# Triangles by ranges of chunks, the product of r and k on VectorE, and a chunk of the recurrence in three blocks

## The chip, the cores and the metric

One Trainium2 chip, one core. The metric is the device time in microseconds (us) of one execution; the kernel before takes 2971.76 us (median of 3 runs, 2968.67 to 2973.62). Engines are named as in the profile: PE (TensorE; PEld are its weight loads), DVE (VectorE), ACT (ScalarE), POOL (GpSimd), SP (the queue that issues most transfers; ACT and POOL issue some of theirs).

## What is computed

One inference step of a two-layer decoder: an RWKV-7 layer and a latent-attention layer, on 1024 prompt tokens and 8 sample tokens. The change touches the first layer alone: its keys and decays, and its recurrence over time.

```python
mixed = h[None] + dx[None] * mix[:4, None, None, :]
r, k, v, z = jnp.einsum('pbtd,pde->pbte', mixed, w_in)
w_log = -jax.nn.softplus(-(w0 + jnp.tanh(xw @ w1) @ w2)) - 0.5
decay = jnp.exp(-jnp.exp(w_log.astype(F32)))
a = jax.nn.sigmoid(a0 + (xa @ a1) @ a2)
kk = heads(k * k_k)                                # then normalised per head
k = k * (1 + (a - 1) * k_a)
...
def _wkv_step(S, inp):
    r, w, k, v, a, b = inp
    sa = jnp.einsum('bhvk,bhk->bhv', S, a)
    S = S * w[:, :, None, :] + sa[..., None] * b[:, :, None, :] + v[..., None] * k[:, :, None, :]
    return S, jnp.einsum('bhvk,bhk->bhv', S, r)
...
bonus = (jnp.sum(rh * kh * r_k, axis=-1, keepdims=True) * vh)
out = ((yn + bonus) * jax.nn.silu(z)) @ w_out
```

There are 32 heads of 64 channels (2048 in all), so 16 tiles of 128 channels hold two heads each. The kernel does the recurrence in 32 chunks of 32 tokens; within a chunk a 32x32 unit triangular matrix per head must be inverted ("the triangle"), and that inverse is the matrix U below.

## The kernel before

**The loop over k** (inside `phase_a`, span 480 to 960 us). `for ct in range(KI - 1)` goes over the 16 tiles. In turn `ct` PE projects k of the tile after (`kproj`, 24 steps of three matmuls p<-mh,w1h / ml,w1h / mh,w1l), projects the decay and the rate (`ua`, six pairs u<-th,l2h and u<-th,l2l, the second over 64 rows alone), forms sums of squares (`norm`, ss), the products inside a chunk of the tile before (`score`, sc), transposes (`rows`, tr) and the bonus (`bonus`, bo<-K,rkb). DVE makes the running decays by two scans (`decay2`, L797 and L798: Wp and its inverse Wi), the new key (`newkey`, L806 to L808) and the scaled rows RA and BK (`raw_rows`, `unit`, `unit2`, `unit_rows`, L813 to L830). The low parts of the split weights come from L76 (w1l on DVE here). POOL forms K<-R,GG, the product of r and the new key (L821), which `bonus` reads in the next turn. Program order is the order of every engine's queue; PE, DVE, ACT and POOL each run theirs in order.

**The triangles.** `inverse(q, ...)` solves eight packs: pack q holds the four heads of tiles 2q and 2q+1 for all 32 chunks, as 128 partitions (head, chunk). It has 31 steps of a product (Xt<-N,X, L1081) and a sum (X<-X,Xt, L1083) over up to 256 elements. `steps` gives one step of the open pack after three of four steps of `kproj`; seven packs run on POOL, one pack per two tiles, and the eighth on DVE after the loop. The results go to `u_d` and, for the last two, to `u2_d`.

**The seam** (960 to 1034 us). After the last `score`, PE has 24 steps of the z projection (`zg`) around the last rows, the transposes boT of the bonus, 27 more z steps, and then rh of chunk 0. DVE splits the mixed rows ml and solves the eighth triangle; POOL stores it.

**The recurrence** (`phase_r`). `for c in range(NC)` has six blocks per chunk: rh (X by state), sa (U by rhs), new_state (s), outs (y), for the first and the second half of the heads (`rh(c,0)`, `new_state(c-1,1)`, `sa(c,0)`+`outs(c-1,1)`, `rh(c,1)`, `new_state(c,0)`, `sa(c,1)`+`outs(c,0)`), each followed by `fill(w)`, which puts in z steps at an even rate so that PE has work while ACT and DVE move the block's result. `load(c+2)` brings the chunk's rows: `xs_d` on SP (64 rows, 16 pieces of 512 bytes each) and `ra_d` on ACT (pieces of 256 bytes). `out_block` normalises four chunks' output, a step per block. `sample_step` does the eight sample tokens on POOL and DVE, one step per block, with the state S fetched and stored in 16 parts.

Of the kernel before, what the change touches and what calls it, by code (L numbers as in the profile page):

```python
# [21 lines left out]
P = 128  # L22
# [33 lines left out]
def tile_yoco(ctx, tc, A, O, dbg=None):  # L56
# [30 lines left out]
    xs_d = scr("xs_d", (2, NC, 64, P * KI))  # L87
# [4 lines left out]
    n_d = scr("n_d", (KI, 2, NC, C, C))  # L92
    mz_d = scr("mz_d", (KT, P, T))
    u_d = scr("u_d", (NC, 4, C, 6, C))
    u2_d = scr("u2_d", (NC, 2, 4, C, C))
# [102 lines left out]
    def phase_a():  # L198
        with ExitStack() as px:
# [15 lines left out]
            shT = lp.tile([P, KT, NB], F32, name="shT")  # L215
# [3 lines left out]
            omx = hp.tile([P, 48], F32, name="omx")  # L219
            w1x = px.enter_context(ExitStack())  # L220
# [399 lines left out]
            Wi = kp.tile([P, NC, 33], F32, name="Wi")  # L620
            E0 = kp.tile([P, NC, 33], BF16, name="E0")
# [6 lines left out]
            G.memset(E0, 0.0)  # L628
            G.memset(E0[:, :, 0:1], 1.0)
# [16 lines left out]
            def wcut(i, ct, hf):  # L646
# [8 lines left out]
                lo(b_, raw[:, 4 * hf:4 * hf + 4], a)  # L655
# [7 lines left out]
            def lora(ct):  # L663
                raw = kp.tile([P, P], F32, tag="l2r", name=f"l2r{ct}")
                SY.dma_start(raw[0:64], A["a_w2"][0][:, ts(ct, P)])
                SY.dma_start(raw[64:128], A["a_a2"][0][:, ts(ct, P)])
                st[ct]["l2r"] = raw

            def lcut(ct):
                raw = st[ct]["l2r"]  # L670
                s2 = st[ct]["s2"] = [kp.tile([P, P], F32R, tag=f"l2h{i}", name=f"l2h{i}_{ct}", bufs=2) for i in range(2)]
                l2 = st[ct]["l2"] = kp.tile([P, P], F32R, tag="l2l", name=f"l2l{ct}", bufs=2)
                for i in range(2):
                    me = slice(64 * i, 64 * i + 64)
# [8 lines left out]
            def ua(ct):  # L683
# [3 lines left out]
                for i, dst in enumerate((d["TW"], d["TA"])):  # L687
                    me = slice(64 * i, 64 * i + 64)
                    for n in range(3):
                        p_ = kbank(f"u{i}_{ct}_{n}")  # L690
                        mm(p_[:, :NQ], d["s2"][i], th2[i][:, nsl[n]], True, False)
                        mm(p_[:, :NQ], d["l2"][me], th2[i][me, nsl[n]], False, True)
# [84 lines left out]
            def norm(ct):  # L777
                d = st[ct]
                RN = d["RN"] = kp.tile([P, T], F32, tag="RN", name=f"RN{ct}")
                for n in range(3):  # L780
                    p_ = kbank(f"ss{ct}_{n}")
                    mm(p_[:, :NQ], blk, d["SQ"][:, nsl[n]], True, True)
                    V.tensor_scalar(RN[:, nsl[n]], p_[:, :NQ], 1e-24, None, ALU.max)
                ACT.activation(RN, RN, AF.Ln)
                ACT.activation(RN, RN, AF.Exp, scale=-0.5)

            def decay(ct):

# [12 lines left out]
            def newkey(ct):  # L801

                d = st[ct]
                TA = d["TA"]
                GG = d["GG"] = kp.tile([P, T], F32, tag="GG", name=f"GG{ct}", bufs=2)
                V.tensor_scalar(GG, TA, dv[:, 2, ct:ct + 1], dv[:, 3, ct:ct + 1], ALU.mult, ALU.add)  # L806
                V.tensor_scalar(TA, TA, -0.5, -0.5, ALU.mult, ALU.add)
# [1965 lines left out]
```

## Time and profile before

| | |
|---|---|
| median of the runs | 2971.76 us |
| the profiled execution | 2943.64 us |
| its span, first to last instruction | 2941.9 us |
| mean granted TensorE clock | 0.957 |
| PE busy | 2696.3 us, 92% |
| DVE busy | 1672.7 us, 57% |
| POOL busy | 1430.5 us, 49% |
| ACT busy | 1361.2 us, 46% |

PE is busy for 92% of the span, so what can be gained lies where it is not, and the stages differ: the same engines are read by stretches further down. A busy share of PE holds time at the lower clock too; a stretch with PEclk below 1 has both idle time and slower matmuls. "Idle before, releaser" names what ended an idle time.

### The profile page before, as it was taken

How to read it: one execution, taken by the hardware profiler on the slowest of the kernel's cores; microseconds unless marked ns; L12 is line 12 of the kernel's file. 1: busy time of each engine (PE TensorE's matmuls, PEld its weight loads, DVE VectorE, ACT ScalarE, POOL GpSimd, SP SyncE). 2: the span in 40 equal slices, each digit the busy share in tenths (PEclk: the TensorE clock that was granted, in tenths of full speed). 3: DMA queues.
4: the chain of work that ended last, by engine and by line, in shares of the span. 5: the costliest groups of instructions: out<-in, count | busy, mean ns of one | idle time of the engine just before them, and what ended most of it. 6: DMA issues, size and time to landing. Idle time of an engine off the chain costs nothing.

```text
span 2941.9 us, 64866 instructions
## 1 busy us (share of the span) xinstructions
PE 2696.3 (92%) x26386; PEld 2418.5 (82%) x26386; DVE 1672.7 (57%) x2952; ACT 1361.2 (46%) x2886; POOL 1430.5 (49%) x1385
## 2 busy tenths in 40 slices
PE   7999998878786788888879999999999999899998
PEld 7999997766675677767769989999999999666897
DVE  7232117989797756666574144127777777533414
ACT  7232226767675444445454335225555555333423
POOL 3322121699999566663245455313444433475342
PEclk9999999989898899999989999999999999999999
DMA  4332334667677899999777552322111111586525
GB/s 157 120 126 76 96 88 113 162 145 174 155 162 190 206 223 218 227 227 210 175 228 225 173 123 78 107 83 83 54 56 54 56 52 55 157 274 201 179 90 187
DMA packets 567501, 423.80 MB, mean 144 GB/s; under 512 B 176260, under 2 KB 515649, under 8 KB 567074
## 3 DMA queue, kind: packets, MB, share of 16 engines
q1 hardware_dynamic: 473954, 336.06, 42.5%
q10 hardware_dynamic: 79648, 38.42, 4.9%
q0 software_dynamic: 13600, 45.16, 4.9%
q8 instruction: 208, 3.41, 0.5%
q14 instruction: 91, 0.75, 0.1%
HBM read 281.69 MB, written 133.35 MB: 141 GB/s over the span
## 4 chain that ended last, share of the span: by engine, by line
PE 57%; POOL 7%; DVE 7%; DMA 5%; issue 4%; ACT 3%; SPq 1%; ACTq 0%; DVEq 0%; POOLq 0%
PE p L62 8%; PE zb L62 6%; PE sc L62 6%; PE bo L62 5%; PE wop L62 4%; PE o L62 4%; POOL Xt L1081 2%; POOL X L1083 2%; PE s L62 2%; PE q L62 2%; PE pt L2156 2%; PE v L62 2%; PE k L62 1%; PE pt L2575 1%; PE bt L62 1%
## 5 line engine op out<-in xcount | busy, mean ns | idle before, releaser
L76 POOL TENSOR_TENSOR wl<-wr,wh 128x1024 fp32r<-128x1024 f32 x32 | 84.3, 2654 | 288.0 <-ACT wh L71 269.5
L1081 POOL TENSOR_TENSOR Xt<-N,X 128x31 f32<-128x31 f32 (+15 forms) x217 | 187.0, 862 | 27.2 <-DMA N<-n_d 11.0
L1083 POOL TENSOR_TENSOR X<-X,Xt 128x31 f32<-128x31 f32 (+15 forms) x217 | 183.8, 847 | 17.0
L71 ACT CAST pth<-pt 128x256 fp32r<-128x256 f32 (+1 forms) x320 | 108.2, 355 | 128.8 <-DVE ptl L76 74.8
L1289 DVE TENSOR_TENSOR st<-s,gC 64x512 f32<-64x512 f32 x128 | 88.2, 689 | 131.6 <-PE s L62 129.2
L62 PE MATMUL p<-mh,w3h 128*128 128x344 f32 x384 | 149.6, 390 | 6.2 <-issue 5.0
L76 DVE TENSOR_TENSOR ptl<-pt,pth 128x256 fp32r<-128x256 f32 (+1 forms) x320 | 120.9, 391 | 27.0 <-ACT pth L71 25.0
L62 PE MATMUL p<-ml,w3h 128*128 128x344 f32 x384 | 130.8, 341 | 5.1 <-issue 2.9
L62 PE MATMUL p<-mh,w1h 128*128 128x344 f32 x360 | 134.9, 375 | 0.0
L62 PE MATMUL p<-mh,w3l 128*128 128x344 f32 x384 | 127.1, 337 | 3.7 <-issue 3.7
L62 PE MATMUL r<-mh,wh 128*128 128x344 f32 x384 | 124.7, 325 | 4.6 <-ACT tf L483 4.6
L62 PE MATMUL r<-mh,wl 128*128 128x344 f32 x384 | 124.1, 323 | 0.0
L62 PE MATMUL r<-ml,wh 128*128 128x344 f32 x384 | 123.9, 323 | 0.0
L2139 ACT ACTIVATE pr<-sc,mx 128x128 f32<-128x128 f32 (+7 forms) x128 | 95.4, 745 | 53.1 <-DVE mx L2136 51.6
L62 PE MATMUL p<-mh,w1l 128*128 128x344 f32 x360 | 119.9, 333 | 0.0
L62 PE MATMUL p<-ml,w1h 128*128 128x344 f32 x360 | 119.8, 333 | 0.0
L2136 DVE TENSOR_REDUCE mx<-sc 128x1 f32<-128x128 f32 (+7 forms) x128 | 96.7, 755 | 3.2
L1305 ACT COPY y<-y 32x256 f32<-32x256 f32 x256 | 93.2, 364 | 10.7 <-PE y L62 7.1
L1276 ACT COPY st<-sa 32x256 f32<-32x256 f32 x128 | 46.4, 362 | 111.1 <-PE sa L62 100.7
L1950 DVE TENSOR_TENSOR zbr<-zb,RS 128x384 f32<-128x384 f32 (+1 forms) x48 | 24.6, 515 | 126.1 <-PE zb L62 123.8
L62 PEld LDWEIGHTS s<-st,xz 128*64 128x64 f32 x2048 | 72.6, 148 | 27.9 <-issue 20.9
L2041 POOL TENSOR_TENSOR qp<-qp,rope 128x256 f32<-128x256 f32 (+1 forms) x30 | 22.4, 747 | 145.8 <-DMA qsw<-qp 122.4
(1237 smaller groups left out, 9944.9 us busy)
## 6 DMA issues: line engine op xcount, KB each, us to landing
xs_d<-XS SPq DMA_DIRECT2D x64, 512.0 KB, 5.9
xz<-xs_d SPq DMA_DIRECT2D x64, 512.0 KB, 9.0
wr<-in_a_w_in_dram SPq DMA_DIRECT2D x17, 1024.0 KB, 6.1
ra_d<-RA SPq DMA_DIRECT2D x32, 512.0 KB, 7.3
xz<-ra_d ACTq DMA_DIRECT2D x58, 256.0 KB, 7.4
rT_d<-rr ACTq DMA_DIRECT2D x16, 516.0 KB, 2.6
R<-rT_d SPq DMA_DIRECT2D x16, 516.0 KB, 3.5
w3r<-in_a_w_in_dram SPq DMA_DIRECT2D x16, 512.0 KB, 6.2
```

Of the source, the lines that this page charges most:

```text
L62: PE.matmul(out, lhsT=lhsT, rhs=rhs, start=start, stop=stop)
L71: ACT.copy(out, in_)
L76: (eng or V).tensor_tensor(out, in_, hi_.bitcast(F32), ALU.subtract)
L1081: eng.tensor_tensor(t3, N_[:, s_:s_ + 1, s_ + 1:].to_broadcast([P, a, b]), X_[:, r0:r1, s_:s_ + 1].to_broadcast([P, a, b]), ALU.mult)
L1083: eng.tensor_tensor(X_[:, r0:r1, s_ + 1:], X_[:, r0:r1, s_ + 1:], t3, ALU.add)
L1276: (V.tensor_copy if j % 2 else ACT.copy)(d, pa[j % 2][ts(j, 32)])
L1289: V.tensor_tensor(ST[s_][1 - c % 2][rows, qs, :], p3[rows], gC[rows, qs, c:c + 1].to_broadcast([64, 8, 64]), ALU.mult)
L1305: ACT.copy(ys[B][ts(ci, 32), a:a + 2].rearrange("p a s d -> p (a s d)"), p_[ts(j, 32), 0:256])
L2136: V.tensor_reduce(mx, sc[:, :W], AX.X, ALU.max, negate=True)
L2139: ACT.activation(pr[:, :W], sc[:, :W], AF.Exp, bias=mx, accum_out=sm)
L2156: PE.transpose(pt[:, ts(q, P)], pr[:, ts(g + q, P)], ident)
L2575: PE.transpose(p_[:, ts(r, P)], pg[:, r, ts(c, P)], ident)
```

## The change

1. **Loop.** r times k goes from POOL to DVE (`rk`, after `unit_rows`); the low part of w1 goes from DVE to POOL. One scan of the summed exponents (CS) takes the place of two, and ACT makes Wp, Wi and gC by Exp; ACT makes the factor of `newkey`; the rate's affine step is folded into `unit2` and `unit_rows`. The second matmul of `ua` reads 128 rows (both halves of th), from doubled raw weights. `rows` copies a transposed bank once (TR) and no longer eight times per pair. The parts of a turn stand in another order; the end of `decay2` and `newkey` now stands at the end of the turn before.
2. **Triangles.** Tiles 0 to 7 stay packs over all chunks, two packs to an instruction, on POOL from turns 4 and 8 at 0.36 steps per z or k step. Tiles 8 to 15 are packs over eight chunks: chunks 0 to 15 on DVE after the loop (two packs to an instruction), chunks 16 to 31 on POOL during the recurrence (`side`), ahead of the sample step.
3. **Scratch.** `xs_d` is two tensors, by tile; a store writes rows of 2 or 4 KB, a load reads pieces of 256 bytes, four loads per chunk on SP in place of two. `u2_d` holds four tensors, stored by 16 transfers each: for the first by SP and ACT in turn, for the second by POOL.
4. **Recurrence.** Three blocks per chunk, with `fill(2.0)` each (6.0 per chunk, as before). The output block has two steps per block; the side work two, and three from chunk 12 on.

```diff
@@ lora, lcut, ua
-                raw = kp.tile([P, P], F32, tag="l2r", name=f"l2r{ct}")
+                raw = kp.tile([P, 2, P], F32, tag="l2r", name=f"l2r{ct}")
...
-                        mm(p_[:, :NQ], d["l2"][me], th2[i][me, nsl[n]], False, True)
+                        mm(p_[:, :NQ], d["l2"][:, i], th2[i][:, nsl[n]], False, True)
@@ wcut
-                lo(b_, raw[:, 4 * hf:4 * hf + 4], a)
+                lo(b_, raw[:, 4 * hf:4 * hf + 4], a, G if i == 1 else V)
@@ decay, decay2
+                ACT.activation(CS[:, :, 1:33], c3(TW), AF.Identity, bias=ones[:, 0:1])
...
-                V.tensor_tensor_scan(fl(Wp), fl(Wp), fl(E0), 0.0, ALU.mult, ALU.add)
-                V.tensor_tensor_scan(fl(Wi), fl(Wi), fl(E0), 0.0, ALU.mult, ALU.add)
-                V.tensor_copy(gC[:, ct, :], Wp[:, :, 32])
+                V.tensor_tensor_scan(fl(CS), fl(E0), fl(CS), 0.0, ALU.mult, ALU.add)
+                ACT.activation(fl(Wp), fl(CS), AF.Exp, scale=-0.5 * CDEC)
+                ACT.activation(Wi, CS[:, :, 1:33], AF.Exp, scale=0.5 * CDEC)
+                ACT.activation(gC[:, ct, :], CS[:, :, 32], AF.Exp, scale=-0.5 * CDEC)
@@ newkey, unit, rk
-                V.tensor_scalar(GG, TA, dv[:, 2, ct:ct + 1], dv[:, 3, ct:ct + 1], ALU.mult, ALU.add)
-                V.tensor_scalar(TA, TA, -0.5, -0.5, ALU.mult, ALU.add)
+                ACT.activation(GG, st[ct]["TA"], AF.Identity, bias=dv[:, 3, ct:ct + 1], scale=dv[:, 2, ct:ct + 1])
-                G.tensor_tensor(d["K"][:, :S], d["R"][:, :S], d["GG"][:, :S], ALU.mult)
+                V.tensor_tensor(d["K"][:, :S], d["R"][:, :S], d["GG"][:, :S], ALU.mult)
@@ rows
-                for u in range(2):
-                    src = slice(64 * u, 64 * u + 64)
-                    ACT.copy(x4[64:128, :, u, :], v4[src, :, 0, :])
-                    ACT.copy(x4[0:64, :, u, :], v4[src, :, 1, :])
+                ACT.copy(d["TR", hf][:, :, ts(g % 2, 4)], p_.rearrange("p (m s d) -> p s m d", m=4, s=2))
...
+                        SY.dma_start(xs_d[1][s_, ct][:, HC[hf]], d["XS", hf][64 * s_:64 * s_ + 64])
+                        for u in range(2):
+                            SY.dma_start(xs_d[0][1 - s_, ct][:, c0 + 8 * u:c0 + 8 * u + 8], d["TR", hf][ts(u, 64), s_])
@@ the loop
+            GROUPS = {4: [(0, 0), (0, 1)], 8: [(0, 2), (0, 3)]}
+            def whole(qs, eng=G):
...
+                rate[0] = 0.36
@@ after the loop
-            iv7 = inverse(KI // 2 - 1, ivb, [(V, 0, C)], late)
-            next(iv7)
+            iv7 = whole([(1, 0), (1, 1)], V)
...
@@ inverse, store
+                            {0: (SY, ACT), 1: (G, G)}.get(q, (SY, SY))[j % 2].dma_start(u2_d[q][:, j, :, x], X_[rows, i])
@@ phase_r, load
-                    SY.dma_start(X[rows, :, 128 - 128 * s_:256 - 128 * s_], xs_d[s_, c].rearrange("r (a t) -> r a t", t=P))
+                    for i, x in enumerate((c // 16 * 16 + c % 2 * 8 + c % 16 // 2, c)):
+                        SY.dma_start(X[rows, :, o + 64 * i:o + 64 * i + 64], xs_d[i][s_, :, :, x].rearrange("a r t -> r a t"))
@@ phase_r, the chunks
-                for i in range(6):
+                for i in range(3):
...
-                    fill(1.4 if i % 3 == 2 else 0.8)
+                    run(take(sg, 3 if c > 11 else 2))
+                    fill(2.0)
```

On POOL in the middle of the loop, before: each product of r and k (L821, K) stands among the steps of a pack of triangles (N, X, Xt).

```order
L1081 TENSOR_TENSOR Xt_5662<-N_5660,X_5661 128x256
L1083 TENSOR_TENSOR X_5661<-X_5661,Xt_5662 128x16x16
L1081 TENSOR_TENSOR Xt_5662<-N_5660,X_5661 128x255
L1083 TENSOR_TENSOR X_5661<-X_5661,Xt_5662 128x17x15
L821 TENSOR_TENSOR K_5452<-R_5695,GG_5841 128x1024
L1081 TENSOR_TENSOR Xt_5662<-N_5660,X_5661 128x252
```

The same place now: a step covers two packs, and what stands among the steps is the low part of the weights of the next k tile (w1l).

```order
L1107 TENSOR_TENSOR Xt_6907<-N_6905,X_6906 128x440
L1109 TENSOR_TENSOR X_6906<-X_6906,Xt_6907 128x2x22x10
L76 TENSOR_TENSOR w1l_0_7786<-w1r_7591,w1h_0_7766 128x512
L1107 TENSOR_TENSOR Xt_6907<-N_6905,X_6906 128x414
L1109 TENSOR_TENSOR X_6906<-X_6906,Xt_6907 128x2x23x9
L1107 TENSOR_TENSOR Xt_6907<-N_6905,X_6906 128x384
L1109 TENSOR_TENSOR X_6906<-X_6906,Xt_6907 128x2x24x8
L76 TENSOR_TENSOR w1l_1_7848<-w1r_7591,w1h_1_7846 128x512
```

K left POOL's queue and w1l came into it, twice a tile. On ACT at the seam, before: the last copies of transposed rows, then the copies of the bonus (bT<-bo), which the transposes boT on PE read, then the z rows.

```order
L872 COPY XS_1_9451<-tr_3_9573 64x4x64
L873 COPY XS_1_9451<-tr_3_9573 64x4x64
L1041 COPY bT<-bo 32x256 x4
L767 COPY zrow_9680<-p_0_0_9384 128x344
L767 COPY zrow_9680<-p_0_1_9388 128x344
L767 COPY zrow_9680<-p_0_2_9392 128x344
```

The same place now: eight stores of the triangle X that DVE solves stand ahead of those copies.

```order
L880 COPY TR_1_9132<-tr_2_9127 128x2x256
L880 COPY TR_1_9132<-tr_3_9134 128x2x256
L1118 DMA u_0_d<-X_9056 8x32x32 x8
L1068 COPY bT<-bo 32x256 x4
L769 COPY zrow_9270<-p_0_0_8941 128x344
L769 COPY zrow_9270<-p_0_1_8945 128x344
```

The first of the eight waits for DVE's last step on X_9056, so bT and the z rows stand behind the whole triangle.

## Rows read from the trace of the kernel before

**Rows 1.** Busy us (and instructions) of PE, PEld, DVE, ACT, POOL by stretch; PEclk, DMA share, GB/s.

```profile
515.30:540.40 25.10, 24.59 (x242) 20.06 (x242) 23.14 (x36) 21.35 (x44) 3.66 (x3) 1.00 0.76 178
...
704.40:774.60 70.20, 52.57 (x486) 42.95 (x486) 64.24 (x78) 45.15 (x88) 65.36 (x67) 0.86 0.62 145
490.90:904.00 413.10, 334.79 (x3147) 271.83 (x3146) 363.75 (x465) 283.90 (x563) 340.97 (x370) 0.91 0.66 156
904.00:960.30 56.30, 46.71 (x501) 39.34 (x502) 43.17 (x53) 30.56 (x64) 52.58 (x55) 0.86 0.88 232
960.30:1034.50 74.20, 54.59 (x661) 46.69 (x660) 47.60 (x86) 37.08 (x78) 36.28 (x56) 0.84 0.85 200
1034.50:1474.60 440.10, 387.14 (x8459) 320.82 (x8459) 278.50 (x477) 210.86 (x539) 232.77 (x158) 0.94 0.91 212
```

**Rows 2.** Waits of PE from 500 to 1050: total us, times, longest.

```profile
PE bo L62 <- POOL K L821: 53.3, 9, 13.7
PE ss L62 <- DVE RN L783: 23.0, 10, 5.0
```

**Rows 3.** PE in order of time in one step of `ua` and `kproj`: start, us.

```profile
553.92 0.32 PE L62 MATMUL u<-th,l2h 128*128 128x344 f32 x1
...
554.79 0.32 PE L62 MATMUL p<-ml,w1h 128*128 128x344 f32 x1
...
555.11 0.32 PE L62 MATMUL u<-th,l2h 128*128 128x344 f32 x1
```

**Rows 4.** DVE in one tile (515.3 to 540.4), groups: busy us, mean ns, idle before.

```profile
L825 DVE TENSOR_TENSOR TA<-TA,RN 128x1032 f32<-128x1032 f32 x1 | 3.4, 3407 | 0.0
...
L798 DVE TENSOR_TENSOR_SCAN Wi<-Wi,E 128x1056 f32<-128x1056 f32 x1 | 2.3, 2330 | 0.0
...
L76 DVE TENSOR_TENSOR w1l<-w1r,w1h 128x512 fp32r<-128x512 f32 x2 | 1.4, 682 | 0.0
...
L808 DVE TENSOR_TENSOR GG<-GG,K 128x1032 f32<-128x1032 f32 x1 | 1.2, 1226 | 0.0
L806 DVE TENSOR_SCALAR GG<-TA,dv 128x1032 f32<-128x1032 f32 x1 | 0.8, 808 | 0.0
L807 DVE TENSOR_SCALAR TA<-TA 128x1032 f32<-128x1032 f32 x1 | 0.7, 699 | 0.0
```

**Rows 5.** POOL in two tiles (645 to 704.4), groups.

```profile
L1081 POOL TENSOR_TENSOR Xt<-N,X 128x252 f32<-128x252 f32 (+15 forms) x32 | 24.7, 771 | 3.2 <-DMA N<-n_d 0.9
...
L821 POOL TENSOR_TENSOR K<-R,GG 128x1024 f32<-128x1024 f32 x2 | 4.7, 2361 | 0.0
```

**Rows 6.** ACT in one tile (515.3 to 540.4), groups.

```profile
L872 ACT COPY XS<-tr 64x256 f32<-64x256 f32 x8 | 2.9, 366 | 0.1
...
L791 ACT ACTIVATE Wi<-TW,cpos 128x1024 f32<-128x1024 f32 x1 | 1.1, 1132 | 0.0
```

**Rows 7.** The seam, DVE in order of time: start, us.

```profile
971.73 0.67 DVE L1081 TENSOR_TENSOR Xt<-N,X 128x31 f32<-128x31 f32 x1
...
995.96 0.40 DVE L1081 TENSOR_TENSOR Xt<-N,X 128x231 f32<-128x231 f32 x1
...
1002.29 0.25 DVE L1083 TENSOR_TENSOR X<-X,Xt 128x87 f32<-128x87 f32 x1
```

**Rows 8.** The seam, PE in order of time: start, us.

```profile
972.44 1.16 PE L1045 MATMUL boT<-ctab,bT 32*128 32x32 f32 x8
```

**Rows 9.** The chain of waits in one chunk: start, us, what.

```profile
1404.83 1.62 PE p L62 x9
...
1407.04 0.68 PE p L62 x3
```

**Rows 10.** DMA queues from 1034.5 to 1474.6: packets, MB, share of 16 engines.

```profile
q1 hardware_dynamic: 111090, 70.71, 68.5%
q10 hardware_dynamic: 63723, 21.39, 21.7%
```

**Rows 11.** POOL from 1034.5 to 1366: one of the seven operations of a sample part.

```profile
L1157 POOL TENSOR_TENSOR tm<-S,vs 128x512 f32<-128x512 f32 x16 | 21.5, 1343 | 73.9 <-DMA S<-in_state_wkv_dram 58.5 <-DMA vb<-v_d 15.4
```

More of the change, by code (lines that the diff above doesn't have):

```diff
@@ L86, in tile_yoco @@
     zT_d = scr("zT_d", (KI, P, T))
-    xs_d = scr("xs_d", (2, NC, 64, P * KI))
+    xs_d = [scr(f"xs{i}_d", (2, KI, 64, NC, 64)) for i in range(2)]
     ra_d = scr("ra_d", (KI, P, NC, 64))
@@ L881, in bonus, with istep @@
                     mm(bo_[ts(i, H), 0:256], rkb[:, ct, :], st[ct]["K"][:, ts(i, 256)], ct == 0, ct == KI - 1)
-            pend, late = [chain()], []
+            iq, late, due, rate = [], [], [0.0], [0.75]
+            def istep():
+                while iq and next(iq[0], end) is end:
+                    iq.pop(0)
             def steps(g, n):
@@ L887, in steps @@
                     next(g, None)
-                    if u % 4 != 3:
-                        next(pend[0], None)
+                    due[0] += rate[0]
+                    while due[0] >= 1:
+                        due[0] -= 1
+                        istep()
             def mz_load(k):
@@ L927, in phase_a @@
                     lora(ct + 2)
+                nm = norm(ct)
                 if p >= 0:
                     score(p, 0)
[L930 to L936 removed]
+                    rows(p, 0)
+                    bonus(p)
+                steps(kpr, 2)
+                run(take(nm, 2))
+                steps(kpr, 1)
+                run(nm)
+                newkey2(ct)
+                if p >= 0:
+                    score(p, 1)
+                    rows(p, 1)
+                steps(kpr, 2)
                 if ct == KI - 2:
                     mz_load(0)
[L939 to L944 removed]
                 raw_rows(ct, 0)
[L946 to L949 removed]
                 unit(ct)
[L951 to L960 removed]
                 unit2(ct)
@@ L963, in phase_a @@
                 ra_store(ct, 0)
+                steps(kpr, 2)
+                if p >= 0:
+                    score(p, 2)
+                    rows(p, 2)
+                steps(kpr, 3)
+                if p >= 0:
+                    score(p, 3)
+                    rows(p, 3)
+                if ct in GROUPS:
+                    iq.append(whole(GROUPS[ct]))
+                if late and not iq:
+                    late.pop(0)()
+                if ct == KI - 2:
+                    mz_load(1)
                 raw_rows(ct, 1)
@@ L966, in phase_a @@
                 ra_store(ct, 1)
+                rk(ct)
                 sample(ct)
                 rload(ct + 1)
+                for u in range(6):
+                    steps(kpr, 1)
+                    next(up)
+                run(up)
+                if ct + 2 < KI:
+                    lcut(ct + 2)
+                decay(ct + 1)
+                steps(kpr, 2)
+                newkey(ct + 1)
+                if ct + 2 < KI:
+                    lcut2(ct + 2)
+                decay2(ct + 1)
                 if ct == KI - 2:
@@ L971, in phase_a @@
                     mz_cut(1, G, G)
-                if ct % 2 == 0 and p >= 0:
-                    pend[0] = fresh
-                for u in range(8):
-                    steps(kpr, 1)
-                    next(up, None)
-                run(kpr)
-                if ct + 2 < KI:
-                    lcut(ct + 2)
-                decay(ct + 1)
-                if ct == KI - 2:
-                    late.pop(0)()
+                steps(kpr, 6)
+                run(kpr)
             p, ct = KI - 2, KI - 1
@@ L989, in phase_a @@
                 mz_load(k)
-            norm(ct)
-            newkey(ct)
-            decay2(ct)
+            run(norm(ct))
+            newkey2(ct)
+            unit(ct)
+            rk(ct)
             rows(p, 0)
@@ L1008, in phase_a @@
             sample(ct)
-            run(pend[0])
-            late[0]()
+            while iq:
+                istep()
+            while late:
+                late.pop(0)()
             bonus(p)
-            ivb = [kp.tile([P, T], F32, tag="K", name="N7", bufs=2)[:, 0:C * C],
-                   kp.tile([P, T], F32, tag="RN", name="X7")[:, 0:C * C]]
             steps(zg, 6)
@@ L1021, in phase_a @@
             ra_store(ct, 0)
-            ivb.append([kp.tile([P, 16, C], F32, tag="nts", name="Xt7").rearrange("p a b -> p (a b)")])
-            iv7 = inverse(KI // 2 - 1, ivb, [(V, 0, C)], late)
-            next(iv7)
+            iv7 = whole([(1, 0), (1, 1)], V)
+            for _ in range(4):
+                next(iv7)
             ra_store(ct, 1)
```

210 lines of the change are left out of this document (102 added, 108 removed).

## The prediction, as it was made before the change ran

> **What bounds the kernel now.** I read the busy times by stretch first [rows 1]. In the loop over k (490.9 to 904.0, thirteen turns, 31.8 us each) PE is busy 334.8 of 413.1 us and its clock is down to 0.91. Two turns show why. In 515.3 to 540.4 no triangle runs: the turn takes 25.1 us and PE is busy for 24.6 of them. From 704.4 to 774.6 POOL is busy for 65.4 of 70.2 us and DVE for 64.2, and a turn takes 35.1. PE's waits say for whom [rows 2]: 53.3 us before the bonus matmul, for POOL's product of r and k, and 23.0 us in `norm`, for DVE; together 76.3 of the 78.3 us that PE is idle there. The product stands in POOL's queue among the triangles, which fill that engine [rows 5]. In the seam (960.3 to 1034.5) PE is idle for 19.6 us of 74.2. In the recurrence (29 chunks from 1034.5 to 1474.6, 15.2 us each) PE is busy for 387.1 of 440.1 us, and the DMA engines for 0.91 of the time.
>
> The sum is made against the profiled execution, 2943.64 us. The median of the runs is 28.1 us (1%) longer; I take the difference over to it unscaled.
>
> **The loop.** PE: one pair of `ua` with the `kproj` step beside it takes 1.19 us (553.92 to 555.11) for five matmuls; two matmuls of equal shape take 0.32 there (554.79 to 555.11) [rows 3]. With 128 rows in all five it is 0.80: 0.39 saved, six times a tile, 2.3 us. `score` and `rows` go from two visits a turn to four, at about 0.25 each: 0.5 back (estimate from [rows 9], where a return to the z matmuls costs 0.2). PE's own time becomes 24.6 - 2.3 + 0.5 = 22.8.
>
> DVE without triangles: of 23.1 go one scan 2.3, two affine steps 0.8 and 0.7, w1l 1.4 [rows 4], and small copies, about 0.9; rk comes at the price of the equal product GG, 1.2; and TA (3.4, beside POOL's product) falls to that price, 2.2 less. That leaves 16.0. Beside triangles DVE took 32.1 a tile, 1.39 times its free 23.1; with that factor on all but the scan, 7.6 goes and 1.7 comes: 26.2. ACT: of 21.4 go sixteen copies of 0.37 (5.9); four wider ones, at twice that price at most, bring 2.9, two affine activations 1.1 each and gC 0.2 [rows 6]: 20.8. POOL: 24 x 0.36 = 8.6 steps a tile; the 31 steps of a pack have 5456 elements, so an instruction on two packs has 352 on average, between 0.77 us (176 elements) [rows 5] and 1.34 (512) [rows 11]: 1.07, times 17.3, plus w1l at 2 x 1.34: 21.2 us. A group's 35 steps last four tiles, two groups eight. POOL's w1l now stands ahead of PE's next `kproj`, behind POOL's steps; with 21.2 of work in a tile its queue does not grow. SP issues about ten more transfers a tile; R and w1r queue behind them, and both have half a tile of slack.
>
> So in five free turns PE is the longest, 22.8; I take 24.5, with 1.7 for banks that wait for `unit_rows` on DVE. In eight loaded turns DVE's 26.2 is the longest; I take 27.5. 5 x 24.5 + 8 x 27.5 = 342.5 against 413.1: **-71** (bounds -110, if every turn is at PE's 23.3, and -36, if a turn still takes 29). From 904.0 to 960.3 PE is idle for 9.6 of 56.3 us and at clock 0.86, and DVE's chain there loses two scans (4.7) and the affine steps: **-12** (-16 to -5).
>
> The Trainium skill (SBUF — State Buffer, "SBUF: two separate sides") says that a DVE instruction with two SBUF inputs and a POOL instruction that reads SBUF lock each other out for a whole instruction. The 3.4 us of TA beside POOL's product agree with that [rows 4]. By it a loaded turn would be no shorter than POOL's work plus DVE's products, which is rival 1.
>
> **The seam.** DVE now solves two packs where it solved one. Its steps cost 0.16 us and 1.04 ns an element (0.40 at 231, 0.25 at 87 [rows 7]) and 0.03 between two: 62 x 0.19 + 4 x 5456 x 1.04 ns = 34.5 us, POOL being idle; before, 31. It starts some 13 us into the stage (11.4 before, 971.73; four more stores go ahead). The stores of the result are what matters: eight stand on ACT ahead of the copies bT and wait for DVE's last step, and PE's boT waits for bT. Before, boT ran 12.1 us into the stage [rows 8] and the 27 z steps behind it hid the triangle. Now it runs at 13 + 34.5 + 3.5 (eight issues) + 1.5 (bT) = 52.5, and PE stands for about 40 us; then come 27 z steps of 0.48 (13.0), and two chunks at 14.7, with 2 for the low clock: 97 against 74.2, **+23**. What is given back is the old start's waiting, 19.6 us idle at clock 0.84. Bounds: +10 if N comes early and stores overlap, +33 if POOL's sixteen stores delay the first states.
>
> **The recurrence.** z matmuls come in runs: nine in 1.62 us, three in 0.68 [rows 9], so 0.157 each and 0.21 for the start of a run. Three runs a chunk fall away: 0.6 x 29 = -18. The loads of `xs_d` go from 2048 packets of 512 bytes a chunk to 4096 of 256. From the two queues [rows 10] a packet costs 43.4 ns at 637 bytes on average and 24.0 at 336 (share x 440.1 us x 16 / packets), on a line 2.3 ns + 0.0645 ns a byte: 0.3 us of the 16 engines per chunk, 0 to +9 over the stage, since they are at 0.91. The sample step is pushed into seventeen chunks. I take **-10** (-25 to +25).
>
> Sum: -71 - 12 + 23 - 10 = -70; 2971.8 - 70 = **2902 us**.
>
> **Rivals.**
> 1. *POOL paces the loaded turns.* POOL's own work without DVE beside it, by DVE's clean slope about twice per element, is near 18 us a tile, DVE's products with two inputs near 10.8; one after the other and with PE waiting for the late w1l, 31 a turn: 8 x 3.5 = +28, 2930. For it: POOL and DVE both filled before. Against: POOL has fewer instructions. 0.12.
> 2. *The squeezed sample step paces the late chunks.* Seven operations of 1.34 and a wait for S (58.5 us over 16 parts, 3.7) make 13.1 us a part [rows 11]; nine steps a chunk are 1.125 parts, 14.7, and the output block's products add 3.2: 17.9 a chunk against 14.6, seventeen times: +56, 2958. Against: a late POOL gives S time to land. 0.10.
> 3. *The loop reaches PE's floor* and the recurrence keeps its 18 and more: -110 - 16 + 18 - 19 = -127, 2845. 0.12.
> 4. *Slower: packets cost by number, not by bytes.* If a 256-byte packet costs what a 512-byte one does (35.3 ns by the line), 2048 more a chunk are 4.5 us of a stage whose DMA engines have 1.4 free: +136 over 30 chunks with nothing else changed, 3038. It turns the sign from 26 ns a packet on, which costs 70 us. Against: the queue that carries mostly 256-byte pieces pays 24.0 ns at 336 bytes. 0.05.
> 5. *The loop's wait is replaced one for one* by DVE or ACT: 2972. 0.03.
>
> The Trainium skill (DMA: Bandwidth & Descriptors, "Specifications") names 512 bytes as the least transfer for full rate, with a read-modify-write below; by that rule rival 4 would be near. The two queues' equal price per byte speaks against it here.
>
> **How the numbers follow.** Forecast 0.58, rivals 0.12, 0.10, 0.12, 0.05, 0.03. A measurement here tells a difference of 0.2% (6 us) from none. Forecast and rivals 1 to 3 are faster; 0.02 is taken off for 1 and 2 together, which end near 2986 (slower 0.01) or near none (same 0.01): faster 0.90, same 0.04, slower 0.06. The range 2848 to 2950 holds the forecast's own bounds and rival 1; it leaves out rival 4, rival 5 and about half of 2 and of 3, 0.19.
>
> **What would show it.** Right: the wait bo<-K is gone and none of its size stands before ss or p; turns of 24 to 28 us; boT starting some 50 us into the seam, with ACT's stores ahead of it; 256-byte packets near 19 ns and chunks of 14 to 15 us. Wrong: p waiting for w1l on POOL (rival 1); DVE's sa waiting for POOL's tm after chunk 12 (rival 2); chunks over 18 us from the first on with the DMA engines full (rival 4). A triangle on DVE that PE does not wait for would make the seam's term wrong.

## The result, and the profile after

The changed kernel takes 3045.66 us (median of 4 runs, 3040.8 to 3049.96) against 2972.69 of the kernel before beside it: 1.0239 times as long, with an interval of 1.0206 to 1.0271. The forecast was 2902; the change is slower. A repeat in another series (below, after2) gave 1.0239 again.

In three of the five series of runs (this one is among them) the stage of the sample tokens' pages took 226 to 237 us in every kernel profiled, in the other two 198 to 202, and the medians of the kernel before differ likewise (2967 to 2973 us there, 2935 to 2941 here), so kernels are compared by ratios inside a series.

The profiled execution of the changed kernel took 3040.8 us, its span is 3038.7 (before: 2943.64 and 2941.9). By landmarks on PE (the same matmul in both traces; the start of the seam to within 1.5 us) the difference of 96.8 us lies so:

| stretch (times of before) | before | after | difference | forecast |
|---|---|---|---|---|
| to the k matmul behind the last bonus of the loop, at 905.0 (after: 838.7) | 905.0 | 838.7 | -66.3 | -71 |
| from there to the seam (960.3; after: about 890.3) | 55.3 | 51.6 | -3.7 | -12 |
| the seam, to chunk 2 (1034.5; after: 1000.6) | 74.2 | 110.3 | +36 | +23 |
| chunks 2 to 30 | 440.1 | 534.8 | +94.7 | -10 |
| the rest | 1467.3 | 1503.3 | +36 | 0 |

Of the last line 31.8 us are the stage of pages, which in the repeat has its old length (199.3 us): not the change's. The stretches of after (columns as in [rows 1]; the first is the thirteen turns of the loop, the second starts at the k matmul):

```profile
484.50:833.60 349.10, 313.86 (x3149) 275.91 (x3148) 284.26 (x332) 244.85 (x428) 202.45 (x154) 0.94 0.66 178
838.70:890.30 51.60, 42.51 (x522) 36.62 (x519) 35.37 (x53) 32.32 (x54) 9.86 (x5) 0.93 0.94 237
890.30:1000.60 110.30, 50.27 (x664) 44.55 (x663) 51.67 (x90) 32.25 (x62) 28.31 (x49) 0.75 0.65 150
1000.60:1175.80 175.20, 130.19 (x2918) 114.02 (x2919) 79.36 (x141) 72.82 (x185) 81.50 (x110) 0.89 0.79 179
1175.80:1535.40 359.60, 259.50 (x5551) 226.72 (x5554) 213.29 (x335) 140.81 (x359) 205.96 (x149) 0.86 0.78 180
```

The loop gained most of what it was to gain: its thirteen turns take 349.1 us in place of 413.1. The recurrence (the last two rows) lost it and more: PE is busy for 389.7 us, about as before (387.1, [rows 1]), but idle for 145 us where it was idle for 53, its granted clock fell from 0.94 to 0.87, and the DMA engines are *less* busy than before, 0.78 against 0.91. The chunks 2 to 11 take 17.5 us each, the later ones 18.9; before, 15.2.

**The loop.** PE's waits in it (total us, times, longest):

```profile
PE u L62 <- ACT nts L861: 20.0, 12, 5.1
PE ss L62 <- ACT nts L861: 5.2, 4, 2.1
PE p L62 <- POOL w1l L76: 4.5, 1, 4.5
```

The 53.3 us before the bonus, for POOL, and the 23.0 in `norm`, for DVE [rows 2], are gone; PE is now idle for 35 us in all, most of it for ACT's copies nts of the products inside a chunk. From one `norm` to the next on PE the turns without triangles take 23.5 to 23.9 us, the eight with them 24.6 to 31.3, 28.9 on average.

**The seam.** Rows of the timelines around PE's wait (start, us; in brackets the idle time and its end):

```profile
904.66 0.22 DVE L1107 TENSOR_TENSOR Xt<-N,X 128x62 f32<-128x62 f32 x1 [5.11 <-DMA N<-n_d]
...
939.14 0.27 DVE L1109 TENSOR_TENSOR X<-X,Xt 128x62 f32<-128x62 f32 x1
939.44 12.09 ACTq L1118 DMA_DIRECT2D u_d<-X  x8
951.57 1.53 ACT L1068 COPY bT<-bo 32x256 f32<-32x256 f32 x4 [52.95 <-DMA u_d<-X]
951.99 1.59 PE L1072 MATMUL boT<-ctab,bT 32*128 32x32 f32 x8 [49.52 <-ACT bT L1068]
```

DVE solves two packs in 34.75 us (forecast 34.5), then ACT's eight stores take 12.1, and PE stands for 49.5 us before boT; before, boT came while the triangle still ran [rows 8].

**The recurrence.** PE's waits in chunks 2 to 30:

```profile
PE ot L1396 <- DVE y L1388: 52.3, 9, 16.3
PE rh L62 <- issue: 33.7, 11, 9.5
PE s L62 <- DVE st L1307: 14.2, 5, 6.0
PE st L1150 <- ACT ozt L1397: 10.1, 2, 8.3
```

Before, PE waited for ot 3.0 us in all, and the two lines of rh were 11.1 (issue) and 5.7 (v).

The line "rh <- issue", whose releaser the profile does not name, is mostly a wait for v. SP loads a chunk's rows of v into st, which rh reads, and each of the four such waits of over 3 us ended 0.1 us after that load had landed. One of them:

```profile
1358.59 1.21 SPq L1282 DMA_DIRECT2D st<-v_d  x1
1360.41 7.87 SPq L1268 DMA_DIRECT2D xz<-xs_d  x4
1367.05 0.39 PE L62 MATMUL rh<-st,xz 128*32 128x64 f32 x2 [9.49 <-issue]
```

The load of v landed at 1366.96. With the line that names v, PE waits for v for some 41 us (before, 17 at most).

ot are the transposes of the output block (ozt is ACT's copy of them), y and vb its rows and the bonus's. One of these waits, followed back through three engines' timelines:

```profile
1246.96 1.26 POOL L1186 TENSOR_TENSOR tm<-S,vs 128x512 f32<-128x512 f32 x1 [11.62 <-DMA S<-in_state_wkv_dram]
1248.18 2.34 POOL L1381 TENSOR_TENSOR y<-y,lnw 128x1024 f32<-128x1024 f32 x1
1250.47 1.90 POOL L1382 TENSOR_TENSOR vb<-vb,bon 128x1024 f32<-128x1024 f32 x1
1252.41 1.73 DVE L1388 TENSOR_TENSOR y<-y,vb 128x512 f32<-128x512 f32 x1 [12.87 <-POOL vb L1382]
1254.20 1.11 PE L1396 MATMUL ot<-ctab,y 128*128 128x128 f32 x4 [10.77 <-DVE y L1388]
```

The sample step's first operation of a part (tm) stands at the head of POOL's queue and waits 11.6 us for S. Behind it stand the output block's two products, behind those DVE's sum, and behind that PE. And S is late because SP is: it issued that load at 1243.26. In total POOL waits for S little longer than before (66.2 us; 58.5 in [rows 11]); what grew is the wait of what stands behind, first after, then before:

```profile
DVE y L1388 <- POOL vb L1382: 70.6, 9, 19.2
```

```profile
DVE y L1357 <- POOL vb L1351: 12.3, 5, 3.9
```

What SP waits for, first after, then before:

```profile
SPq L1268 <- DMA xz<-ra_d: 32.2, 9, 7.6
SPq L1283 <- DMA xz<-ra_d: 30.4, 9, 6.5
SPq L1282 <- PE y L62: 25.7, 12, 6.6
```

```profile
SPq L1251 <- PE y L62: 98.1, 25, 11.8
```

The wait for y is slack: SP is early and waits for a free buffer. It fell from 98.1 to 25.7 us; in its place SP waits for transfers that ACT issued for the same chunk. (In the traces the transfers of SP and ACT take eight semaphores in turn, in program order, and each waits for its own to be free, so until the eighth before it has landed, whichever queue carries it.) The theories to tell apart were therefore: **A**, POOL's queue, crowded by the side work, makes the output block late; **B**, twice as many pieces in the loads of `xs_d` make SP late; and **C**, that three blocks a chunk leave too little work on PE to cover ACT and DVE.

### The profile page after: what moved, and what is told of

It reads as the page before. It is cut to its first block, busy times and chain, and to the rows that moved or that the text cites. A ratio compares the mean times of both kernels' runs of the same rounds, so it can differ in the third digit from the quotient of the medians.

```text
span 3038.7 us, 64902 instructions
## 1 busy us (share of the span) xinstructions
PE 2676.5 (88%) x26386; PEld 2442.0 (80%) x26386; DVE 1593.7 (52%) x2794; ACT 1320.3 (43%) x2726; POOL 1296.6 (43%) x1216
## 4 chain that ended last, share of the span: by engine, by line
PE 48%; DMA 7%; DVE 6%; POOL 4%; issue 4%; ACT 3%; SPq 2%; another core or an unknown queue 1%; ACTq 1%; DVEq 0%; POOLq 0%
PE zb L62 6%; PE sc L62 6%; PE bo L62 5%; PE wop L62 4%; PE o L62 4%; PE p L62 3%; PE q L62 2%; PE pt L2200 2%; PE pt L2619 2%; PE v L62 2%; PE ssc L62 1%; PE k L62 1%; PE bt L62 1%; PE s L62 1%; PE cq L62 1%
## 5 line engine op out<-in xcount | busy, mean ns | idle before, releaser
L62 PE MATMUL p<-mh,w3h 128*128 128x344 f32 x384 | 143.0, 373 | 2.6 <-issue 1.6
L76 POOL TENSOR_TENSOR w1l<-w1r,w1h 128x512 fp32r<-128x512 f32 x30 | 49.9, 1664 | 150.5 <-ACT w1h L71 125.8
L62 PE MATMUL s<-st,xz 128*64 128x64 f32 x2048 | 88.5, 243 | 16.5 <-DVE st L1307 14.2
L2552 POOL DMA_INDIRECT pg<-in_cache_ckv_dram,idx x64 | 60.8, 949 | 95.4 <-issue 43.4
L62 PE MATMUL rh<-st,xz 128*32 128x64 f32 x2048 | 53.8, 235 | 53.2 <-issue 33.7
L2180 DVE TENSOR_REDUCE mx<-sc 128x1 f32<-128x128 f32 (+7 forms) x128 | 96.8, 756 | 3.2
```

Source lines behind the costliest of these rows:

```text
L62: PE.matmul(out, lhsT=lhsT, rhs=rhs, start=start, stop=stop)
L76: (eng or V).tensor_tensor(out, in_, hi_.bitcast(F32), ALU.subtract)
L2180: V.tensor_reduce(mx, sc[:, :W], AX.X, ALU.max, negate=True)
L2552: G.indirect_dma_start(t_.rearrange("p r c -> p (r c)"), None, A[nm].rearrange("n (q r) c -> (n q) (r c)", r=4), off)
```

## The experiments

Times of stages are from the profiled execution of each kernel, "chunks 2 to 30" from the first rh of chunk 2 to that of chunk 31 on PE: 440.1 before, 534.8 after. The ratios are to the kernel before in the same series. The expectations of the first four put numbers on the scale of 2972 for the kernel before; their series had 2941.

**rate7**

```diff
-                    run(take(sg, 3 if c > 11 else 2))
+                    run(take(sg, 3 if i == 2 else 2))
```

> The changed kernel with seven steps of side work per chunk in every chunk (2, 2, 3) in place of six up to chunk 11 and nine from chunk 12 on. Theory A (POOL's queue: the output block's products, for which PE's transposes ot wait, stand behind side steps that wait for a transfer, and nine steps a chunk leave the load of S less time): the chunks from 12 on, 19.5 us each now, fall by 2 to 3 us, the first twelve rise by under 1, the recurrence is 30 to 50 us shorter and the time about 3005. Theory B (twice as many packets for the loads of the chunk's rows make every transfer on SP late): within 10 us of 3045. Theory C (three blocks a chunk expose the latencies of ACT and DVE): within 10 us of 3045.

518.0 us, ratio 1.0157 (1.0109 to 1.0204). The chunks from 12 on fell from 18.9 to 17.4, the first ones rose from 17.5 to 18.7. A's sign and about half of its size (30 to 50 us).

**p512**

```diff
-    xs_d = [scr(f"xs{i}_d", (2, KI, 64, NC, 64)) for i in range(2)]
+    xs_d = scr("xs_d", (2, NC, 64, P * KI))
...
-                    for i, x in enumerate((c // 16 * 16 + c % 2 * 8 + c % 16 // 2, c)):
-                        SY.dma_start(X[rows, :, o + 64 * i:o + 64 * i + 64], xs_d[i][s_, :, :, x].rearrange("a r t -> r a t"))
+                    SY.dma_start(X[rows, :, o:o + P], xs_d[s_, c].rearrange("r (a t) -> r a t", t=P))
```

> The changed kernel with the scratch of the rows in its old layout: the loads of the recurrence read pieces of 512 bytes again in two transfers a chunk, and the stores in the loop over k write pieces of 256 bytes in their place. Theory A (POOL's queue): the recurrence stays above 515 us of its 535, the loop gets 5 to 30 us longer from the stores, time 3040 to 3075. Theory B (packets): the recurrence falls to 440 to 470 us, time about 2975 to 3000. Theory C: as A.

483.8 us, ratio 1.0062 (1.0039 to 1.0085): between the ranges of A and B, nearer to B. Up to boT, where only the smaller stores differ, the kernel is 9 us longer. SP has its slack again:

```profile
SPq L1283 <- PE y L62: 98.9, 23, 7.5
```

So the loads as laid out carry 51 us of the 95, and A alone does not explain the loss.

**obdve**

```diff
-                G.tensor_tensor(yf, yf, lnw[:, ts(hf, 1024)], ALU.mult)
+                V.tensor_tensor(yf, yf, lnw[:, ts(hf, 1024)], ALU.mult)
```

and the same for y less m and for vb by bon.

> The changed kernel with the output block's three products per half (y less its mean, y by lnw, vb by bon) on DVE in place of POOL. Theory A: PE's waits ot<-DVE y, 52.3 us now, fall below 10, DVE takes about 1.8 us a chunk more, the stores of the output and with them the loads of v and S on SP come earlier, the recurrence is 50 to 80 us shorter, time 2965 to 2995. Theory B: the waits move to rh (for xz), the recurrence is shorter by under 20 us. Theory C: shorter by under 20 us, or longer, since DVE has more to do in a block.

507.6 us, ratio 1.0119 (1.0077 to 1.016): 27 us shorter, less than A's 50 to 80. The waits for ot are gone, as A says, but about half of the gain is lost to a longer wait for DVE (6.7 us before this edit):

```profile
PE rh L62 <- DVE st L1320: 47.9, 30, 8.3
```

**six**

```diff
-                for i in range(3):
+                for i in range(6):
...
-                    run(take(sg, 3 if c > 11 else 2))
-                    fill(2.0)
+                    run(take(sg, 2 if c > 11 and i % 2 else 1))
+                    fill(1.4 if i % 3 == 2 else 0.8)
```

> The changed kernel with the six blocks per chunk of the kernel before in the recurrence (one step of the output block and one or, from chunk 12 on, in turn one and two of the side work in each); all else as changed. Theory C: the recurrence falls to 440 to 460 us, time 2960 to 2980. Theory A: the same number of steps of side work per chunk, only spread, so the waits for POOL shrink by a half at most: 10 to 40 us shorter, time 3005 to 3035. Theory B: within 15 us of 3045.

503.1 us, ratio 1.0125 (1.0079 to 1.017): inside A's bounds, far from C's. The edit also spreads the side work more evenly, so it does not tell the two apart alone; combo9six below does.

**after2**: the changed kernel again.

> The changed kernel once more, as it is, as the mark for the others of this call: 1.024 times the kernel before, with 530 to 540 us from chunk 2 to chunk 31. If the 32 us more in the sample tokens' attention (from its first page to the last projection 231 us against 200 before) belong to the change they stand here again; if they were that execution's own, the stage takes 198 to 202 us and the ratio is 1.010 to 1.015.

Ratio 1.0239 (1.0198 to 1.0279), 533.1 us, and 199.3 us in the stage of pages: neither alternative as it was written. The 32 us were not the change's, and the ratio stands; that the kernel before has the long stage in the first series too is inferred from its medians.

**p512x4** and **p256x4** take B apart: transfers, pieces, or the distance between pieces.

Each load of p512 is cut into two, in p512x4 by tiles (512 pieces of 512 bytes each),

```diff
-                    SY.dma_start(X[rows, :, o:o + P], xs_d[s_, c].rearrange("r (a t) -> r a t", t=P))
+                    for i in range(2):
+                        SY.dma_start(X[rows, 8 * i:8 * i + 8, o:o + P], xs_d[s_, c].rearrange("r (a t) -> r a t", t=P)[:, 8 * i:8 * i + 8])
```

and in p256x4 by the halves of each piece (1024 pieces of 256 bytes each):

```diff
+                        SY.dma_start(X[rows, :, o + 64 * i:o + 64 * i + 64], xs_d[s_, c].rearrange("r (a t) -> r a t", t=P)[:, :, 64 * i:64 * i + 64])
```

> p512 with each of its two loads of 512-byte pieces cut into two of half the tiles: as many transfers per chunk as the changed kernel, as few and as large packets as before. Theory B1 (the number of packets delays the loads): as p512, 475 to 492 us from chunk 2 to 31. Theory B2 (the number of transfers: SP holds a transfer back until an earlier one has landed, as its waits SPq<-DMA xz<-ra_d, 32.9 us in the changed kernel, suggest): 505 to 530 us, 25 to 45 us over p512, and those waits are back.

> The scratch of the rows in the old layout as in p512, but each load cut the other way, by the two halves of a 512-byte piece: four transfers a chunk of 1024 pieces of 256 bytes, as many and as small as in the changed kernel, whose pieces however lie 8 KB apart where here all of a chunk lies in one block. Theory P (the number of pieces): 520 to 540 us from chunk 2 to 31, as the changed kernel (533 and 535). Theory Q (how far apart the pieces lie): 460 to 490, as p512 and p512x4 (484 and 466).

p512x4: 466.4 us, ratio 1.0048 (1.0031 to 1.0066). p256x4: 533.4 us, ratio 1.0256 (1.0232 to 1.0281). The two have the same transfers in the same order from the same scratch and differ in the pieces alone: 67 us. Cutting p512's loads in two cost nothing (466.4 against 483.8; why it is even less stays open, and the ratios of the whole do not tell them apart), so the number of transfers is not it. Nor is it that the pieces lie 8 KB apart in the changed kernel, since in p256x4 they do not. In p256x4 SP's waits are those of the changed kernel:

```profile
SPq L1286 <- DMA xz<-ra_d: 32.6, 9, 5.9
SPq L1270 <- DMA xz<-ra_d: 31.0, 8, 6.0
SPq L1285 <- PE y L62: 20.3, 11, 5.1
```

**xact**

```diff
-                        SY.dma_start(X[rows, :, o + 64 * i:o + 64 * i + 64], xs_d[i][s_, :, :, x].rearrange("a r t -> r a t"))
+                        (ACT if c > 2 and i else SY).dma_start(X[rows, :, o + 64 * i:o + 64 * i + 64], xs_d[i][s_, :, :, x].rearrange("a r t -> r a t"))
```

> The changed kernel with the loads from the second of the two tensors issued by ACT in place of SP, from chunk 3 on: pieces and layout as changed, SP's queue carries half of them. Theory R (the cost is in SP's queue, in which U, S and the next v stand behind the four loads): 470 to 505 us from chunk 2 to 31. Theories P and Q: 520 to 540.

513.9 us, ratio 1.0161 (1.0136 to 1.0185): between the two. SP has 120.0 us of slack (SPq L1282 <- PE y), POOL's wait for S is halved (66.2 to 33.5), and the delay went to the other issuer:

```profile
PE ot L1396 <- ACT ozt L1397: 38.2, 11, 9.6
```

**rasp**

```diff
-                    (ACT if c > 2 else SY).dma_start(X[rows, :, 64 + 128 * s_:128 + 128 * s_], ra_d[:, rows, c].rearrange("a r t -> r a t"))
+                    SY.dma_start(X[rows, :, 64 + 128 * s_:128 + 128 * s_], ra_d[:, rows, c].rearrange("a r t -> r a t"))
```

> The changed kernel with the loads of ra issued by SP, too, in place of ACT: pieces and layout as changed, six of a chunk's loads in one queue, and no transfer of SP that waits for one of ACT's loads. Theory L (the cost of 256-byte pieces comes about through SP's waits for ACT's loads xz<-ra_d, 95 us in p256x4, because SP runs some 6 us behind ACT): 465 to 500 us from chunk 2 to 31. Theory I (SP's own time to issue them, 4.3 us a chunk against 2.9 and 1.7): 530 to 560, since SP now issues two more.

562.7 us, ratio 1.033 (1.0304 to 1.0357). That is just above theory I's range and far from L's, but L is not refuted by it: the waits for ra are gone, and waits for ACT's z rows stand in their place.

```profile
SPq L1283 <- DMA zT_d<-zrow: 30.3, 5, 7.9
SPq L1344 <- DMA zT_d<-zrow: 28.7, 5, 11.7
```

What the runs show is that the cost moves with whoever issues the pieces, and grows with what stands in one queue. Added up over SP's timeline, the issues of `xs_d` take 42.7 us in the kernel before (56 of 0.76), 122.9 after (115 of 1.07), 82.3 in p512x4 (114 of 0.72). The loads themselves are not slower: by the semaphores' last steps a chunk's load of `xs_d` is through some 10 us after its first issue in the changed kernel, 11 in the other two (medians). They start late, and so does what stands behind them: PE's waits of rh without a name and for v come to 41.1 us in the changed kernel, 39.5 in p256x4 and 61.7 in c9x256 (below), against 8.8 in p512x4 and 19.4 in combo9, which has its loads. SP issues it 6 us after ACT's ra of the same chunk in the changed kernel, and 1 us after in before, p512 and p512x4. How much of the 67 us is the issuing itself and how much the waits for ACT that follow from being late stays open, and so does why an issue of small pieces is long at times.

**combo, combo7, combo8, combo9** put the parts together, with the seam mended. combo is p512 and obdve, combo7 p512 and rate7, both with the first group's stores all on SP; combo8 is p512x4 and rate7 with those stores on POOL:

```diff
-                            {0: (SY, ACT), 1: (G, G)}.get(q, (SY, SY))[j % 2].dma_start(u2_d[q][:, j, :, x], X_[rows, i])
+                            {0: G, 1: G}.get(q, SY).dma_start(u2_d[q][:, j, :, x], X_[rows, i])
```

> p512 and obdve together, and the first group's sixteen stores of the triangle all on SP in place of SP and ACT in turn. If the two delays add (POOL's queue 24 us, the loads 51): 445 to 465 us from chunk 2 to 31. If DVE becomes the bound in its place: 470 to 485. The seam: PE's wait for bT, 49.5 us, falls below 10; what comes last then is the triangle itself, so that the first sa waits for U, and from boT to chunk 2 it takes 30 us more, 15 to 30 us less in all. Time 0.98 to 1.00 of before.

> p512, rate7 and the stores of the first group on SP: the output block stays on POOL, with seven steps of side work in every chunk. If POOL's queue delays the output block by the steps in a row (three per block from chunk 12 on): 455 to 475 us from chunk 2 to 31, near combo. If by the transfers that POOL waits for: 475 to 490, as p512. The seam as in combo. Time 0.985 to 1.005 of before.

> p512x4 and rate7, and the first group's stores of the triangle all on POOL, so that neither the copies bT on ACT nor the loads of v on SP stand behind DVE's last step of the triangle (in combo and combo7, with the stores on SP, PE's wait for bT had gone and a wait of 47 to 48 us for v had come in its place). From the turn's start to chunk 2 20 to 30 us less than combo7 (its 1004.9 to about 980), then 445 to 460 us from chunk 2 to 31. Time 0.980 to 0.992 of before. If what comes last in the seam is the triangle and U, the wait moves to sa<-U and stays under 30 us.

> combo8, and what POOL's queue waits for at the borders of its side work taken away: two buffers for X of the side triangles, their N and the sample's v4 fetched by POOL itself, three empty steps before v4 is used. POOL's waits Xr<-u_d (25.6 us in combo7) and v<-vs_d (21.3) go. If the output block behind them holds PE: 5 to 15 us less than combo8 from chunk 2 to 31; if not, within 4 us of it.

combo9's edit on top of combo8, in short:

```diff
-                        bufs = [vp.tile([P, 1, C * C // x], F32, tag=t_, name=f"{t_}r{r}") for t_, x in (("N", 1), ("X", 1), ("Xt", 4))]
+                        bufs = [vp.tile([P, 1, C * C // x], F32, tag=t_, name=f"{t_}r{r}", bufs=2 if t_ == "X" else 1) for t_, x in (("N", 1), ("X", 1), ("Xt", 4))]
...
-            SY.dma_start(v4[:, g], vs_d[g, 0:NB].rearrange("b (q x) -> (b q) x", x=P))
+            G.dma_start(v4[:, g], vs_d[g, 0:NB].rearrange("b (q x) -> (b q) x", x=P))
+        for g in range(3):
+            yield
```

and the load of N for the side triangles goes from SP to POOL likewise.

combo: 482.5 us, 1.0061 (1.0031 to 1.0091): obdve adds nothing to p512. combo7: 457.4 us, 0.9981 (0.9961 to 1.0001). combo8: 438.7 us, 0.9894 (0.987 to 0.9918). combo9: 444.0 us, 0.987 (0.9847 to 0.9894): in the recurrence 5 us more than combo8, not the 5 to 15 less of an output block held by POOL's waits at the borders of its side work, and the ratios' intervals overlap; those waits cost nothing that can be seen once the rest is mended. With the stores on SP the seam had gained nothing, since the loads of v stand behind them there; with them on POOL v and U are late by less, 29.6 us together, and chunk 2 starts at 994.4 (combo7: 1004.9), where about 980 was expected. PE in the seam of combo7, then of combo8:

```profile
PE rh L62 <- DMA st<-v_d: 46.7, 1, 46.7
```

```profile
PE rh L62 <- DMA st<-v_d: 17.0, 4, 12.2
PE sa L62 <- DMA U<-u_d: 12.6, 1, 12.6
```

**combo9six** and **c9x256** each change one thing in combo9: six blocks a chunk in place of three, with seven steps of side work as there; and the changed kernel's scratch and loads in place of p512x4's.

> combo9 with six blocks a chunk in the recurrence (one step of the output block in each, and one or, in the last, two of the side work). If three runs of z fewer are worth the 0.6 us a chunk that were forecast, and nothing else hides it: 455 to 465 us from chunk 2 to 31 against 444, PE busy 385 to 392 against 374. If the idle time takes it back: 438 to 450.

> combo9 with the changed kernel's scratch and loads (256-byte pieces, four transfers): the last of its parts that combo9 had undone. If the pieces cost the same with POOL's queue and the seam mended: 500 to 520 us from chunk 2 to 31 against 444, time 1.008 to 1.016 of before. If the cost came only together with the crowded queue of POOL: 455 to 475, time 0.990 to 1.000.

combo9six: 428.7 us, ratio 0.9859 (0.9837 to 0.988), the lowest of all, though not clear of combo9; below both ranges of its expectation. c9x256: 498.3 us, ratio 1.0054 (1.0034 to 1.0075), just under the range for pieces that cost the same, and clear of the other. The recurrence of combo9, combo9six and c9x256 as one stretch each (columns as in [rows 1]):

```profile
997.40:1441.40 444.00, 374.28 (x8464) 327.10 (x8463) 296.66 (x475) 213.32 (x544) 293.30 (x262) 0.93 0.92 215
```

```profile
997.00:1425.70 428.70, 378.70 (x8460) 312.23 (x8459) 299.19 (x474) 212.41 (x546) 289.04 (x262) 0.97 0.95 222
```

```profile
985.40:1483.70 498.30, 382.72 (x8463) 337.40 (x8463) 289.56 (x473) 213.07 (x543) 291.85 (x265) 0.89 0.82 192
```

Read upwards from the fastest, the recurrence is 429; three blocks make it 444 (+15 in these two profiles, but only 3, within the intervals, by the ratios of the whole); pieces of 256 bytes 498 (+54, and 55 by the ratios); the side work at six and nine steps a chunk, its border waits on POOL and the stores on ACT 533 (+35, the repeat). With these undone and the seam mended, the rest of the change is worth 1.4% against the kernel before.

## Why the prediction was wrong, step by step

- **The loop, -71: right in its steps, 7 us short.** The thirteen turns gained 64, and 2 came ahead of them. Free turns take 23.5 to 23.9 (forecast 24.5, PE alone 22.8), loaded ones 28.9 (27.5; rival 1 had 31): two errors of opposite sign, -4 and +11. In the loaded turns PE waits for ACT's nts, and ACT for DVE's XS ahead of it, so the chain through DVE is what holds it there, as forecast. From 605 to 834, where PE is idle for 27.8 us:

```profile
PE u L62 <- ACT nts L861: 17.7, 8, 5.1
ACT nts L861 <- DVE XS L860: 46.1, 8, 7.8
```

  POOL is dearer than summed, too: in the eight turns an instruction of a two-pack step takes 1.25 us, where 1.07 was put, and w1l 1.7 against 1.34. The wait that rival 1 asked for, p for w1l, is there once, with 4.5 us. POOL's groups from 605 to 665, beside DVE:

```profile
L1109 POOL TENSOR_TENSOR X<-X,Xt 128x414 f32<-128x414 f32 (+8 forms) x16 | 25.2, 1575 | 1.3
L1107 POOL TENSOR_TENSOR Xt<-N,X 128x414 f32<-128x414 f32 (+8 forms) x16 | 24.8, 1547 | 0.9
L76 POOL TENSOR_TENSOR w1l<-w1r,w1h 128x512 fp32r<-128x512 f32 x4 | 6.1, 1528 | 3.0 <-ACT w1h L71 3.0
```

- **904 to 960, -12: wrong by 8.** PE is idle there for 9.1 us where it was idle for 9.6: its wait for DVE's BK fell from 4.9 us to 1.0, but a wait for ACT's nts came in its place (u, 3.7), and the rest is spread over ACT and DVE. What was gained, 3.7 us, goes with the clock (0.93, before 0.87).
- **The seam, +23: the mechanism right, the size short, +36.** The triangle took what it was to take. The stores took 12.1 us where 3.5 were put: 1.5 us each beside those of SP and POOL, not 0.44. boT ran some 61 us into the seam (forecast 52.5), and what came behind it took 4 us more than put, about what PE waited for U there (3.4).
- **The recurrence, -10: the step that failed.** Three terms of it were wrong, all on the same side: the loads, the three blocks and the side work.

*The loads.* The forecast priced the pieces on the 16 DMA engines alone, 0 to +9 us, and it got that price right. The packets of SP's queue in chunks 2 to 30 of after (packets, MB, share of 16 engines):

```profile
q1 hardware_dynamic: 177264, 73.23, 59.8%
```

That is 0.598 x 534.8 x 16 / 177264 = 28.9 ns at 413 bytes, and the line through [rows 10] gives 2.3 + 0.0645 x 413 = 28.9. But the engines were not the limit (0.78 busy). What the pieces cost is time in the queue that issues them, 80 us more on SP over the stage (40 of them in p512x4 too, which has as many transfers and does not suffer), and that queue also carries S, v and U, for which POOL and PE then wait. By p512x4 against p256x4 the pieces cost the stage 67 us, by combo9 against c9x256 54. SP's issues had no term in the sum, though [rows 11] showed POOL waiting for S.

*Three blocks.* The forecast's 18 us of PE time are there: busy time by clock is 374.3 x 0.93 = 348 us in combo9 against 378.7 x 0.97 = 367 in combo9six, 19 less (an estimate, since the clock is a mean). They bring nothing, because PE is idle for 69.7 us in place of 50.0 and its clock is lower; the ratios of the two kernels, 0.9870 and 0.9859, leave no room, by their intervals, for a gain of 18 us either. That the z steps between the blocks were the cover for ACT and DVE is the likely reason, and not shown.

*The side work.* This was rival 2, priced at +56 on the late chunks with a chance of 0.10 and half outside the range. At 18.9 us the late chunks even passed its 17.9, but most of that is the loads; what its own undoing gives is 15 to 28 us (rate7 against after2, combo7 against p512, combo8 against p512x4; the last two also moved the stores of the seam). Its sign, DVE's sa waiting for POOL's tm after chunk 12, is there with 15.1 us (6.2 before in the whole stage), but the larger cost came by PE's wait for the output block behind tm, which it counted only as POOL time.

- **Rival 4 had the time, 3038, by luck.** It asked for full DMA engines, and they had room; its sum also took all of the 4.5 us a chunk, though it gave the engines 1.4 free (the rest, 3.1, would have made it about 2995). The Trainium skill's rule that went with it (DMA: Bandwidth & Descriptors, "Specifications": 512 bytes as the least transfer for full rate) agrees with p512x4 against p256x4 in that 256 bytes are dearer than 512, by 67 us (no run has a size between), but not as to what is lost there: a packet took 29.0 ns at 413 bytes on average in SP's queue of p256x4 and 42.1 at 621 in that of p512x4, both within 0.3 ns of the line of [rows 10].
- **The range.** The terms of the recurrence had bounds of -25 to +25 that came from DMA packets alone. A change that doubles a queue's issues, and adds work in a queue on which others depend, needs a bound from that queue's own slack: SP's 98 us of waiting for y were the number to read: 3.4 us a chunk, and the added issues alone take 2.8.

## What to carry to other kernels

Price a transfer three times: on the DMA engines, in the queue that issues it, and for what stands behind it in that queue; a layout that makes the stores large and the loads small moves cost to the loads, and their queue may have no slack for it. Work put into an in-order queue as "side work" is only free as long as none of it waits for a transfer ahead of something that another engine waits for; spread it evenly, and fetch its data early. Where an engine is called the bound, fewer of its instructions help only if it does not stand idle in their place.

## What was not expected of the hardware

- An issue on SP of 1024 pieces of 256 bytes takes 1.07 us on average (1.04 in p256x4, median 0.75 and up to 4.4), of 512 pieces of 512 bytes 0.72, of 1024 pieces of 512 bytes 0.76 to 0.86. The engines' time per packet did not rise with small pieces. Nor is the issue's time the pieces' alone: in xact, with half of the loads on ACT, SP's issues of the same 256-byte pieces took 0.83.
- Eight stores of 32 KB by ACT took 12.1 us when SP and POOL stored at the same time; PE's granted clock was 0.75 over the seam.
